# Start of a two-layer hybrid encoder: products of ones ahead on TensorE, a full-row norm spread, one transfer queue, and the second token tile's split ahead of k's casts

## The chip, the cores and the metric

The kernel runs on one core of a Trainium2 chip. The metric is the device time of one execution in microseconds (us). The kernel before took 761.21 us (median of 3 executions, 759.78 to 761.6). All places in time below are microseconds from the start of the profiled span.

## The reference

Two layers (`DEPTH` 2) work on 256 tokens of 1024 channels in float32. Each layer normalises its input, projects it with one matrix of 10,272 columns, sends the segments through a gated delta branch and a differential attention branch, merges both and adds the result to the input. A last norm closes it.

```
def rmsnorm(x, w):
    y = xf * lax.rsqrt(jnp.mean(xf * xf, axis=-1, keepdims=True) + EPS)
    return y.astype(x.dtype) * w

for l in range(DEPTH):
    h = rmsnorm(x, norm_w[l])
    proj = h @ w_in[l]                     # q_a k_a v_a ab_a z_a q_b k_b v_b z_b gates
    ...
    x = x + merged @ w_out[l]
return rmsnorm(x, final_norm_w)
```

The change touches only the norm of the tokens and the first projections behind it (`v_b`, the 32 columns `ab_a`, then `k_a`).

## The kernel before, in words

The 256 tokens are two tiles of 128 (`m` = 0 and 1), one token per partition; `xt[i][:, m]` holds half `i` (512 channels) of tile `m`. A projection needs float32 accuracy, so each operand is cut into a rounded part `hi` and a remainder `lo`, and each product is three matmuls (hi·hi, hi·lo, lo·hi). Weights come in pieces `kp` of 256 rows by 512 columns (512 KB): a transfer to `raw` (L249), a cast on ScalarE to `hi` (L253, "CAST") and a subtraction on VectorE to `lo` (L255).

**The norm of one tile** (`normed`, L192). ScalarE squares both halves with a running sum (L189), GpSimd adds the two sums and EPS (L184) and takes the power -0.5 (L185), and VectorE multiplies tokens, this factor and the norm weight (L199, once per half, tile `h_n`). `norm_row` (L159) supplies the norm weight on all partitions for layer 0: it loads one row of 1024 numbers to partition 0 and multiplies it, on TensorE, with a row of ones (`tri[0:1, 0, :]`, the first row of an upper triangle that GpSimd makes at L114 to L116) into two banks `wb` (L165).

**The split of one tile** (`split_T`, L204). TensorE transposes `h_n` in eight blocks (L209, bank `pt_h`), ScalarE copies four at a time to `hT` hi (L215), and VectorE subtracts to `hT` lo (L216).

**The order around the change.** Layer 0 starts with `v_b`, first half of its columns: `proj_by_tile` (L286) runs all 8 `kt` blocks for token tile 0 and then the same 8 for tile 1. The four weight pieces sit in the buffers `wA`, `wktm`, `wvtm` and `wB` (pieces 0 to 3) and are used twice. `between(kt)` (L389) puts the second token tile's transfers and norm among the pieces of the first pass. Behind that come the 16 small products of `ab_a` (`abp`, L503, weights `wabr`, L498 and L499) and `k_a` (`proj_fm`, L314, banks `pf_k`, weights `hi_k` and `lo_k`).

A scheduler fixes the order on each engine when the program is built. `behind(ins)` and `tc.issue_after(ins)` keep an instruction behind another; `later[kp]` does this for the cast and the subtraction of piece `kp`, `mark["later"]` for those of the next `proj_fm`, and `held[kp]` for its transfer, which then goes to ScalarE's queue if the instruction it is held behind runs there. Each engine works strictly in its order. `raw` has three buffers in turn; pieces named in `spare` take one of two others instead. SyncE (SP) issues the transfers of its queue in order and waits where a buffer isn't free yet.

Of the kernel before, what the change touches and what calls it, by code (L numbers as in the profile page):

```python
# [17 lines left out]
P = 128  # L18
# [31 lines left out]
def hybrid_encoder(  # L50
# [108 lines left out]
    def norm_row(w_row, nm):  # L159

        row = work.tile([P, DM], F32, tag="w4c", name=f"wr_{nm}", bufs=4)
        nc.scalar.dma_start(out=row[0:1, :], in_=w_row.unsqueeze(0))
        wb = [bank(f"wb_{nm}{i}") for i in range(2)]
        for i in range(2):
            T.matmul(wb[i], tri[0:1, 0, :], row[0:1, 512 * i : 512 * i + 512], start=True, stop=True)  # L165
        return wb

    def norm_weights(w_row, nm):
# [9 lines left out]
    def norm_factor(xt_, m, h, r, ss, halves_, after=None):  # L178


        for i in halves_:
            with behind(after):
                sq = mark["square", m, i] = square(xt_, m, h, ss, i)
        G.tensor_scalar(r, ss[:, 0:1], ss[:, 1:2], EPS, ALU.add, ALU.add)  # L184
        mark["pow"] = G.tensor_tensor(r, r, mhalf[:, :1], ALU.pow).ins  # L185
        return sq

# [155 lines left out]


    U_ = big.tile([P, 2, 16, P], F32, name="U_")
    wb = norm_row(norm_w[0], "n0")
    xt = e4("xt0", "ex")
    xdr = x[0].rearrange("(m p) (i d) -> p i m d", p=P, i=2)
# [18 lines left out]
    for l in range(DEPTH):  # L367
# [18 lines left out]
        if l == 0:  # L386
            later[0] = None, mark["norm", 0][1]

            def between(kt):  # L389
                if kt == 2:  # L390
                    held[1] = mark["square", 0, 0]
                    later[1] = mark["split", 0, 0]
                elif kt == 4:
                    tokens(1, mark["square", 0, 1])
                    held[2] = mark["vb00", 0][0]
                elif kt == 6:
                    prenorm(1, xt, wb, 0, (mark["split", 0, 1][0], mark["vb00", 2][1]))
                    later[3] = None, mark["norm", 1][1]
        else:
            later = {1: mark["norm", 0], 2: (mark["norm", 0][0], mark["split", 0, 0][1]), 3: mark["split", 0, 0]}  # L400
            mark["later"] = {0: mark["norm", 1], 1: mark["norm", 1]}
        for _ in proj_by_tile(hT, wl, C_VB, evac_v(0), f"vb{l}0", places, later=later,
                              spare=(1, 3) if l else (), held=held, between=between,
                              turn=lambda m: None if m or not l else mark["turn", 1, 0]):
            pass
        if l == 0:
            norms = mark["pow"]
            with tc.issue_after(norms):
                G.memset(U_, 0.0)
            pos_f = const.tile([P, NM], F32, name="pos_f")  # L410
            with tc.issue_after(mark["norm", 1][1]):
                V.tensor_copy(pos_f, pos_i)
            freq = const.tile([P, RD], F32, name="freq")
            for i, f in enumerate(INV_FREQ):
                V.memset(freq[:, i : i + 1], f)
            angs = const.tile([P, 2, NM, RD], F32, name="angs")
            ang, ang2 = angs[:, 0], angs[:, 1]
            for m in range(NM):
                V.tensor_scalar(ang[:, m, :], freq, pos_f[:, m : m + 1], None, ALU.mult)
            turns = const.tile([P, NM, RD], F32, name="turns")  # L420
            turns_i = const.tile([P, NM, RD], I32, name="turns_i")
            V.tensor_scalar(turns, ang, 1.0 / (2.0 * math.pi), None, ALU.mult)
            V.tensor_copy(turns_i, turns)
            V.tensor_copy(turns, turns_i)
            for c in (TWO_PI_A, TWO_PI_B, TWO_PI_C):
                V.scalar_tensor_tensor(ang, turns, -c, ang, ALU.mult, ALU.add)
            PI_IN = 3.1415925
            V.tensor_scalar(ang, ang, PI_IN, -PI_IN, ALU.min, ALU.max)
            sincos = const.tile([P, 2, NM, RD], F32, name="sincos")
            sin, cos = sincos[:, 0], sincos[:, 1]  # L430
            over = const.tile([P, NM, RD], F32, name="over")
            V.tensor_scalar(ang2, ang, math.pi / 2, None, ALU.add)
            V.tensor_scalar(over, ang2, math.pi, None, ALU.is_gt)
            V.scalar_tensor_tensor(ang2, over, -2.0 * math.pi, ang2, ALU.mult, ALU.add)
            V.tensor_scalar(ang2, ang2, PI_IN, -PI_IN, ALU.min, ALU.max)
# [55 lines left out]


        wab = work.tile([P, KT, 32], F32, tag="w2a", name=f"wab{l}", bufs=2)
        with behind(None if l else mark["vb00", 2][0]):
            (nc.sync if l else nc.scalar).dma_start(
                out=wab, in_=wl[:, C_AB : C_AB + 32].rearrange("(k p) c -> p k c", p=P))
        wabr = work.tile([P, KT, 64], F32R, tag="w2c", name=f"wabr{l}", bufs=3)
        S.copy(wabr[:, :, 0:32], wab)  # L498
        V.tensor_tensor(wabr[:, :, 32:64], wab, wabr[:, :, 0:32].bitcast(F32), ALU.subtract)  # L499
        abp = ps_p.tile([P, 512], F32, tag="p", name=f"abp{l}")  # L500
        for kt in range(KT):
# [700 lines left out]
```

## Time and profile before

| | |
|---|---|
| profiled execution, own time | 761.66 us |
| its span (first to last instruction) | 759.9 us |
| around the span | 1.8 us |
| median of three executions | 761.21 us |
| TensorE busy | 745.7 us, 98% |
| VectorE, ScalarE, GpSimd busy | 575.6, 471.0, 124.2 us |
| moved by DMA | 131.24 MB, 173 GB/s |

PE is TensorE's matmul row, PEld its weight loads, DVE is VectorE, ACT ScalarE, POOL GpSimd and SP SyncE; a "q" behind the name marks an engine's issue of transfers. A row of the timeline has start, length, engine, line, operation, what is written <- what is read, partitions x elements, the count of merged instructions, and in brackets the idle time ahead and what ended it. Float32 matmuls that are not rounded show as two records each (the two products of the norm row are "x4").

### The profile page before, as it was taken

Reading aid. Unit: us, or ns where it says so; the run is one execution under the profiler, and the core shown is the slowest. Engines: PE = TensorE matmul, PEld = TensorE weight load, DVE = VectorE, ACT = ScalarE, POOL = GpSimd, SP = SyncE. Lnnn points to the kernel's source line nnn. Section 1 sums busy time; section 2 is a strip of 40 time slices with the busy share of each in tenths; the row PEclk is TensorE's granted clock in tenths of the full one; section 3 lists DMA queues with packets and bytes.
Section 4 is the critical chain, followed back from the end, with each engine's and each line's share of the span. In section 5 each row is a group of like instructions: output and inputs, shape, how many; then the busy total and the mean of one; then the engine's idle time right before and its main releaser. Section 6 shows DMA issues by size and latency. Waiting matters only on the chain. (4 is left out here: it accounts for less than half of the span.)

```text
span 759.9 us, 13759 instructions
## 1 busy us (share of the span) xinstructions
PE 745.7 (98%) x5158; PEld 640.3 (84%) x5158; DVE 575.6 (76%) x1083; ACT 471.0 (62%) x1012; POOL 124.2 (16%) x187
## 2 busy tenths in 40 slices
PE   7999999999999999999999999999999999999996
PEld 4899889977788889988889889889777888998784
DVE  5686999999886764487577779999989668436782
ACT  5657675667787574645545577665777757465551
POOL 5100451111113130000010025202110410201000
PEclk9999999999999999999999999999999999999999
DMA  7662677776668342557674347768656834335541
GB/s 232 214 204 63 199 225 203 220 199 199 188 195 176 90 137 84 167 192 230 215 228 136 88 140 254 202 195 229 188 167 194 195 113 142 103 111 205 193 139 55
DMA packets 71795, 131.24 MB, mean 173 GB/s; under 512 B 12288, under 2 KB 12752, under 8 KB 71729
## 3 DMA queue, kind: packets, MB, share of 16 engines
q1 hardware_dynamic: 62718, 111.94, 48.8%
q0 software_dynamic: 6304, 15.15, 7.4%
q10 hardware_dynamic: 2706, 3.28, 1.3%
q8 instruction: 40, 0.66, 0.4%
q14 instruction: 27, 0.21, 0.1%
HBM read 123.44 MB, written 6.91 MB: 172 GB/s over the span
## 5 line engine op out<-in xcount | busy, mean ns | idle before, releaser
L270 PE MATMUL pp_qk<-lo_qk,hT 128*128 128x512 f32 x128 | 50.7, 396 | 0.2
L271 PE MATMUL pp_qk<-hi_qk,hT 128*128 128x512 f32 x128 | 50.0, 391 | 0.0
L255 DVE TENSOR_TENSOR lo_qk<-raw_qk,hi_qk 128x1024 fp32r<-128x1024 f32 x32 | 39.6, 1239 | 9.6 <-ACT hi_qk L253 9.3
L269 PE MATMUL pp_qk<-hi_qk,hT 128*128 128x512 f32 x128 | 45.1, 393 | 0.0
L253 ACT CAST hi_qk<-raw_qk 128x1024 fp32r<-128x1024 f32 x28 | 29.4, 1049 | 24.6 <-PE pp_qk L271 12.1
L926 ACT ACTIVATE es<-sc,mx 128x256 f32<-128x256 f32 x64 | 29.7, 475 | 20.7 <-DVE mx L924 20.7
L255 DVE TENSOR_TENSOR lo_pb<-raw_pb,hi_pb 128x1024 fp32r<-128x1024 f32 x16 | 19.6, 1227 | 23.0 <-ACT hi_pb L253 22.9
L327 PE MATMUL pf_q<-hT,hi_q 128*128 128x256 f32 x128 | 36.2, 286 | 0.0
L325 PE MATMUL pf_q<-hT,hi_q 128*128 128x256 f32 x128 | 36.1, 287 | 0.0
L325 PE MATMUL pf_v<-hT,hi_v 128*128 128x256 f32 x128 | 35.9, 285 | 0.0
L327 PE MATMUL pf_v<-hT,hi_v 128*128 128x256 f32 x128 | 35.8, 284 | 0.0
L325 PE MATMUL pf_k<-hT,hi_k 128*128 128x256 f32 x128 | 35.7, 284 | 0.0
L327 PE MATMUL pf_k<-hT,hi_k 128*128 128x256 f32 x128 | 35.6, 283 | 0.0
L255 DVE TENSOR_TENSOR lo_ga<-raw_ga,hi_ga 128x1024 fp32r<-128x1024 f32 x16 | 19.5, 1219 | 20.9 <-ACT hi_ga L253 20.9
L329 PE MATMUL pf_q<-hT,lo_q 128*128 128x256 f32 x128 | 34.8, 285 | 0.0
L329 PE MATMUL pf_v<-hT,lo_v 128*128 128x256 f32 x128 | 34.6, 288 | 0.0
L329 PE MATMUL pf_k<-hT,lo_k 128*128 128x256 f32 x128 | 34.4, 284 | 0.0
L554 DVE SCALAR_TENSOR_TENSOR cvq<-pf_q,cw,cvq 128x254 f32<-128x254 f32 (+1 forms) x64 | 29.9, 477 | 1.9 <-ACT cvq L550 1.4
L253 ACT CAST hi_pa<-raw_pa 128x1024 fp32r<-128x1024 f32 x16 | 16.9, 1054 | 22.8 <-PE pp_pa L271 16.7
L554 DVE SCALAR_TENSOR_TENSOR cvv<-pf_v,cw,cvv 128x254 f32<-128x254 f32 (+1 forms) x64 | 30.0, 476 | 0.1
L554 DVE SCALAR_TENSOR_TENSOR cvk<-pf_k,cw,cvk 128x254 f32<-128x254 f32 (+1 forms) x64 | 28.5, 478 | 2.0 <-ACT cvk L550 1.3
L270 PEld LDWEIGHTS pp_qk<-lo_qk,hT 128*128 128x128 f32 x128 | 24.0, 188 | 6.5 <-DVE lo_qk L255 1.7
(372 smaller groups left out, 2520.2 us busy)
## 6 DMA issues: line engine op xcount, KB each, us to landing
raw_qk<-in_w_in_dram SPq DMA_DIRECT2D x32, 512.0 KB, 4.1
raw_k<-in_w_in_dram SPq DMA_DIRECT2D x16, 512.0 KB, 4.7
raw_q<-in_w_in_dram SPq DMA_DIRECT2D x16, 512.0 KB, 3.8
raw_v<-in_w_in_dram SPq DMA_DIRECT2D x16, 512.0 KB, 3.8
raw_zb<-in_w_in_dram SPq DMA_DIRECT2D x16, 512.0 KB, 3.8
raw_za<-in_w_in_dram SPq DMA_DIRECT2D x16, 512.0 KB, 3.8
raw_ga<-in_w_in_dram SPq DMA_DIRECT2D x16, 512.0 KB, 4.0
raw_pb<-in_w_pb_dram SPq DMA_DIRECT2D x16, 512.0 KB, 4.1
```

The costliest lines, as they stand in the source:

```text
L253: high = (V.tensor_copy if kp in turned else S.copy)(hi[:, :, :n], raw[:, :, :n]).ins
L255: mark[nm, kp] = high, V.tensor_tensor(lo[:, :, :n], raw[:, :, :n], hi[:, :, :n].bitcast(F32), ALU.subtract).ins
L269: T.matmul(o, act[kt // 4][:, 0, kt % 4, ts_], hi, start=kt == 0, stop=False)
L270: T.matmul(o, act[kt // 4][:, 0, kt % 4, ts_], lo, start=False, stop=False)
L271: mark["proj"] = T.matmul(o, act[kt // 4][:, 1, kt % 4, ts_], hi, start=False, stop=kt == KT - 1).ins
L325: T.matmul(o, hi[:, cs], act[kt // 4][:, 0, kt % 4, :], start=first, stop=False, skip_group_check=True)
L327: T.matmul(o, hi[:, cs], act[kt // 4][:, 1, kt % 4, :], start=False, stop=False, skip_group_check=True)
L329: T.matmul(o, lo[:, cs], act[kt // 4][:, 0, kt % 4, :], start=False, stop=done, skip_group_check=True)
L554: V.scalar_tensor_tensor(ca[:, o0:o1], acc[:, b, o0 + sft : o1 + sft], cw[:, j, cb : cb + 1], ca[:, o0:o1], ALU.mult, ALU.add)
L926: S.activation(es[:, n, qt, :], spv[:, qt, :], AF.Exp, bias=mx[:, n, qt : qt + 1], accum_out=s_all[:, h, n, qt : qt + 1])
```

## The change

1. `ones` (128x128, filled on VectorE) and eight float32 products of it with itself stand first on TensorE; nothing reads their bank.
2. The norm row's tile is filled with zeros on VectorE first (128x1024); the row's transfer overwrites partition 0, and the two spreading products take all 128 rows (with the whole `tri[:, 0, :]`, whose column sums give the row again, as all other rows are zero). Both keep their place in the program.
3. The norm's addition of the two sums moves from GpSimd to VectorE (L184). This helper serves both tiles of both layers and the last norm.
4. Second token tile, weight pieces 1 and 2 of `v_b` and the weights `wab` of `ab_a` lose their `held` entries and go to SP's queue. Piece 3 takes a spare buffer, so `raw` starts its second turn one piece later.
5. Piece 2's cast is put behind tile 0's second split; the second tile's squares go behind piece 2's cast alone (its product stays behind piece 2's subtraction), and k's first cast and subtraction, `pos_f` and the cast of `wab` go behind the second tile's last split.

```diff
     def norm_row(w_row, nm):
         row = work.tile([P, DM], F32, tag="w4c", name=f"wr_{nm}", bufs=4)
+        V.memset(row, 0.0)
         nc.scalar.dma_start(out=row[0:1, :], in_=w_row.unsqueeze(0))
...
-            T.matmul(wb[i], tri[0:1, 0, :], row[0:1, 512 * i : 512 * i + 512], start=True, stop=True)
+            mm = T.matmul(wb[i], tri[:, 0, :], row[:, 512 * i : 512 * i + 512], start=True, stop=True)
+            tc.keep_in_program_order(mm)
...
-        G.tensor_scalar(r, ss[:, 0:1], ss[:, 1:2], EPS, ALU.add, ALU.add)
+        V.tensor_scalar(r, ss[:, 0:1], ss[:, 1:2], EPS, ALU.add, ALU.add)
...
+    ones = work.tile([P, P], F32, tag="sqj", name="ones", bufs=1)
+    V.memset(ones, 1.0)
+    idle = bank_c("idle")
+    for _ in range(8):
+        mm = T.matmul(idle[:, :P], ones, ones, start=True, stop=True)
+        tc.keep_in_program_order(mm)
     wb = norm_row(norm_w[0], "n0")
...
                 if kt == 2:
-                    held[1] = mark["square", 0, 0]
                     later[1] = mark["split", 0, 0]
                 elif kt == 4:
-                    tokens(1, mark["square", 0, 1])
-                    held[2] = mark["vb00", 0][0]
+                    tokens(1)
+                    later[2] = mark["split", 0, 1]
                 elif kt == 6:
-                    prenorm(1, xt, wb, 0, (mark["split", 0, 1][0], mark["vb00", 2][1]))
+                    prenorm(1, xt, wb, 0, mark["vb00", 2])
                     later[3] = None, mark["norm", 1][1]
+                    mark["later"] = {0: mark["split", 1, 1]}
...
-                              spare=(1, 3) if l else (), held=held, between=between,
+                              spare=(1, 3) if l else (3,), held=held, between=between,
...
-            with tc.issue_after(mark["norm", 1][1]):
+            with tc.issue_after(mark["split", 1, 1][1]):
                 V.tensor_copy(pos_f, pos_i)
...
-        with behind(None if l else mark["vb00", 2][0]):
-            (nc.sync if l else nc.scalar).dma_start(
-                out=wab, in_=wl[:, C_AB : C_AB + 32].rearrange("(k p) c -> p k c", p=P))
+        nc.sync.dma_start(out=wab, in_=wl[:, C_AB : C_AB + 32].rearrange("(k p) c -> p k c", p=P))
...
-        S.copy(wabr[:, :, 0:32], wab)
+        with behind(None if l else mark["split", 1, 1][0]):
+            S.copy(wabr[:, :, 0:32], wab)
```

What the scheduler makes of it differs from the order before at three places; everything else stands in the same order on every engine, apart from the addition of item 3, which leaves GpSimd and joins VectorE at every norm.

**The first transfers.** SP's queue from its start, before. `xt` are the tokens of tile 0, `raw_vb` the pieces 0 and 3 of `v_b`, `cwr` the convolution weights, `raw_k` the pieces of `k_a`; the tokens of tile 1, pieces 1 and 2 and `wab` stand in ScalarE's queue, among its casts.

```order
L353 DMA xt_0_103<-in_x_dram 128x512
L353 DMA xt_1_104<-in_x_dram 128x512
L249 DMA raw_vb_143<-in_w_in_dram 128x2x512
L439 DMA cwr_264<-in_conv_w_dram 120x128
L249 DMA raw_vb_198<-in_w_in_dram 128x2x512
L249 DMA raw_k_362<-in_w_in_dram 128x2x512
L249 DMA raw_k_392<-in_w_in_dram 128x2x512
```

The same queue of the changed kernel:

```order
L361 DMA xt_0_115<-in_x_dram 128x512
L361 DMA xt_1_116<-in_x_dram 128x512
L251 DMA raw_vb_155<-in_w_in_dram 128x2x512
L251 DMA raw_vb_165<-in_w_in_dram 128x2x512
L361 DMA xt_0_115<-in_x_dram 128x512
L361 DMA xt_1_116<-in_x_dram 128x512
L251 DMA raw_vb_177<-in_w_in_dram 128x2x512
L251 DMA raw_vb_210<-in_w_in_dram 128x2x512
L447 DMA cwr_276<-in_conv_w_dram 120x128
L502 DMA wab_296<-in_w_in_dram 128x8x32
L251 DMA raw_k_374<-in_w_in_dram 128x2x512
```

The second pair of `xt` rows are the tokens of tile 1. All first transfers except the norm row now stand in this one queue, in the order in which they are used; ScalarE's queue keeps the norm row and, later, two pieces of the second half of `v_b`.

**The second token tile.** VectorE's order before, from the subtraction of piece 2 (`wvtm`) to that of k's second piece; `h_n` is the second tile's product, `hT` its split, `wabr` and `angs` are small work for `ab_a` and the rotary angles.

```order
L255 TENSOR_TENSOR wvtm_vb_136<-raw_vb_165,wvtm_vb_136 128x1024
L199 SCALAR_TENSOR_TENSOR h_n_175<-xt_0_103,xr_n_176,wb_n_99 128x512
L199 SCALAR_TENSOR_TENSOR h_n_175<-xt_1_104,xr_n_176,wb_n_100 128x512
L412 CAST pos_f<-pos_i 128x2
L255 TENSOR_TENSOR wB_vb_137<-raw_vb_198,wB_vb_137 128x1024
L499 TENSOR_TENSOR wabr_286<-wab_284,wabr_286 128x8x32
L419 TENSOR_SCALAR angs<-freq,pos_f 128x8
L255 TENSOR_TENSOR lo_k_361<-raw_k_362,hi_k_360 128x1024
L419 TENSOR_SCALAR angs<-freq,pos_f 128x8
L216 TENSOR_TENSOR hT_0_107<-pt_h_184,hT_0_107 128x4x128
L216 TENSOR_TENSOR hT_1_108<-pt_h_191,hT_1_108 128x4x128
L255 TENSOR_TENSOR lo_k_391<-raw_k_392,hi_k_390 128x1024
```

The same stretch of VectorE in the changed kernel:

```order
L257 TENSOR_TENSOR wvtm_vb_148<-raw_vb_177,wvtm_vb_148 128x1024
L186 TENSOR_SCALAR xr_n_188<-xss_n_189 128x1
L201 SCALAR_TENSOR_TENSOR h_n_187<-xt_0_115,xr_n_188,wb_n_111 128x512
L201 SCALAR_TENSOR_TENSOR h_n_187<-xt_1_116,xr_n_188,wb_n_112 128x512
L257 TENSOR_TENSOR wB_vb_149<-raw_vb_210,wB_vb_149 128x1024
L218 TENSOR_TENSOR hT_0_119<-pt_h_196,hT_0_119 128x4x128
L218 TENSOR_TENSOR hT_1_120<-pt_h_203,hT_1_120 128x4x128
L420 CAST pos_f<-pos_i 128x2
L257 TENSOR_TENSOR lo_k_373<-raw_k_374,hi_k_372 128x1024
L427 TENSOR_SCALAR angs<-freq,pos_f 128x8 x2
L257 TENSOR_TENSOR lo_k_403<-raw_k_404,hi_k_402 128x1024
L506 TENSOR_TENSOR wabr_298<-wab_296,wabr_298 128x8x32
```

The split of the second tile moved ahead of `lo_k`, `wabr` and the angles; the norm's addition (L186) now stands on VectorE, behind the subtraction of piece 2. ScalarE's casts follow: the second tile's squares now stand behind the cast of piece 2, the two copies to `hT` ahead of k's casts. On TensorE the order of the two passes stays, but the 16 `abp` products, which stood in three groups among the second pass, now stand in one group behind it.

**The start of layer 1.** VectorE's order before around the norm of tile 1 there (`wB` is a weight piece of `v_b`, `hT_1` the second half of tile 0's split, `lo_k` the first pieces of `k_a`):

```order
L255 TENSOR_TENSOR wB_vb_4130<-raw_vb_4148,wB_vb_4130 128x1024
L216 TENSOR_TENSOR hT_1_4007<-pt_h_4068,hT_1_4007 128x4x128
L199 SCALAR_TENSOR_TENSOR h_n_4100<-xt_0_3924,xr_n_4101,wb_n_4002 128x512
L199 SCALAR_TENSOR_TENSOR h_n_4100<-xt_1_3925,xr_n_4101,wb_n_4002 128x512
L255 TENSOR_TENSOR lo_k_4298<-raw_k_4299,hi_k_4297 128x1024
L255 TENSOR_TENSOR lo_k_4328<-raw_k_4329,hi_k_4327 128x1024
L216 TENSOR_TENSOR hT_0_4006<-pt_h_4109,hT_0_4006 128x4x128
```

And in the changed kernel:

```order
L257 TENSOR_TENSOR wB_vb_4142<-raw_vb_4160,wB_vb_4142 128x1024
L218 TENSOR_TENSOR hT_1_4019<-pt_h_4080,hT_1_4019 128x4x128
L186 TENSOR_SCALAR xr_n_4113<-xss_n_4114 128x1
L201 SCALAR_TENSOR_TENSOR h_n_4112<-xt_0_3936,xr_n_4113,wb_n_4014 128x512
L201 SCALAR_TENSOR_TENSOR h_n_4112<-xt_1_3937,xr_n_4113,wb_n_4014 128x512
L257 TENSOR_TENSOR lo_k_4310<-raw_k_4311,hi_k_4309 128x1024
L257 TENSOR_TENSOR lo_k_4340<-raw_k_4341,hi_k_4339 128x1024
L218 TENSOR_TENSOR hT_0_4018<-pt_h_4121,hT_0_4018 128x4x128
```

Only the addition joined the row; it comes behind the subtraction for `hT_1` in VectorE's queue, where GpSimd had it in a queue of its own.

## The prediction

> **What bounds the kernel now.** I read the page's busy times first, then the busy times by stage, then the timeline of the first 28 us. From the page:
>
> ```profile
> PE 745.7 (98%) x5158; PEld 640.3 (84%) x5158; DVE 575.6 (76%) x1083; ACT 471.0 (62%) x1012; POOL 124.2 (16%) x187
> ```
>
> And by stage (length, then the busy time of PE, PEld, DVE, ACT and POOL, the clock, the DMA share and GB/s):
>
> ```profile
> 0.00:28.00 28.00, 22.86 (x87) 15.52 (x87) 15.62 (x40) 15.12 (x26) 12.62 (x26) 1.00 0.76 237
> 28.00:380.00 352.00, 351.69 (x2489) 304.77 (x2488) 273.47 (x515) 225.72 (x489) 54.57 (x78) 1.00 0.60 177
> 380.00:392.00 12.00, 11.82 (x61) 9.30 (x60) 11.59 (x14) 7.36 (x12) 2.14 (x4) 1.00 0.65 192
> ```
>
> From 28 to 380 us TensorE is idle for 0.3 us of 352, and the order there is unchanged but for the norm's addition. So whatever the change gains or loses before the first product of `k_a` moves the rest of layer 0 as a whole. The idle time to be had stands in the first 28 us, and a busy PE there is not yet one at full pace. The timeline of the first tile:
>
> ```profile
> 0.80 0.52 ACTq L162 DMA_DIRECT2D wr_n<-in_norm_w_dram  x1
> 0.86 0.26 DVE L415 MEMSET freq<- 128x1 f32 x8 [0.86 <-PEq L1190]
> 1.35 1.28 ACT L189 ACT_TABLE_LOAD   x1 [1.35 <-PEq L1190]
> 3.10 3.78 PE L165 MATMUL wb_n<-wr_n,tri 1*128 1x512 f32 x4 [3.10 <-POOL tri L116]
> 3.85 0.63 ACT L189 ACTIVATE h_n<-xt 128x512 f32<-128x512 f32 x1 [1.21 <-DMA xt<-in_x_dram]
> 5.32 0.30 POOL L184 TENSOR_SCALAR xr_n<-xss_n 128x1 f32<-128x1 f32 x1 [2.03 <-ACT h_n L189]
> 5.71 0.57 POOL L185 TENSOR_TENSOR xr_n<-xr_n,mhalf 128x1 f32<-128x1 f32 x1
> 6.31 1.41 DVE L199 SCALAR_TENSOR_TENSOR h_n<-xt,xr_n,wb_n 128x512 f32<-128x512 f32 x2 [3.22 <-POOL xr_n L185]
> 7.69 1.04 ACT L253 CAST wA_vb<-raw_vb 128x1024 fp32r<-128x1024 f32 x1 [2.48 <-DMA raw_vb<-in_w_in_dram]
> 8.77 1.23 DVE L255 TENSOR_TENSOR wA_vb<-raw_vb,wA_vb 128x1024 fp32r<-128x1024 f32 x1 [1.05 <-ACT wA_vb L253]
> 9.28 3.45 PE L309 MATMUL pp_vb<-wA_vb,hT 128*128 128x512 f32 x6 [0.20 <-ACT hT L215]
> 9.91 0.68 DVE L216 TENSOR_TENSOR hT<-pt_h,hT 128x512 fp32r<-128x512 f32 x1
> ```
>
> The first projection waits for piece 0 of its weights (7.69), whose cast and subtraction end at 10.0. The second tile:
>
> ```profile
> 12.15 1.03 ACT L253 CAST wvtm_vb<-raw_vb 128x1024 fp32r<-128x1024 f32 x1
> 13.22 1.23 DVE L255 TENSOR_TENSOR wvtm_vb<-raw_vb,wvtm_vb 128x1024 fp32r<-128x1024 f32 x1 [0.82 <-ACT wvtm_vb L253]
> 14.36 1.40 DVE L199 SCALAR_TENSOR_TENSOR h_n<-xt,xr_n,wb_n 128x512 f32<-128x512 f32 x2
> 15.75 1.22 DVE L255 TENSOR_TENSOR wB_vb<-raw_vb,wB_vb 128x1024 fp32r<-128x1024 f32 x1
> 17.02 1.42 PE L309 MATMUL pp_vb<-wB_vb,hT 128*128 128x512 f32 x5
> 18.88 1.22 DVE L255 TENSOR_TENSOR lo_k<-raw_k,hi_k 128x1024 fp32r<-128x1024 f32 x1 [0.38 <-ACT hi_k L253]
> 19.39 0.73 PE L309 MATMUL pp_vb<-wA_vb,hT 128*128 128x512 f32 x2 [0.94 <-ACT hT L215]
> 20.16 1.28 DVE L216 TENSOR_TENSOR hT<-pt_h,hT 128x512 fp32r<-128x512 f32 x2
> 20.90 1.19 PE L309 MATMUL pp_vb<-wA_vb,hT 128*128 128x512 f32 x4 [0.66 <-DVE hT L216]
> 21.93 1.54 PE L309 MATMUL pp_vb<-wktm_vb,hT 128*128 128x512 f32 x6
> 27.08 0.97 PE L503 MATMUL abp<-hT,wabr 128*64 128x256 f32 x7
> 27.88 0.28 PE L325 MATMUL pf_k<-hT,hi_k 128*128 128x256 f32 x1
> ```
>
> The second pass begins at 19.39 and stalls again at 20.90, both times for `hT`, which stands behind `lo_k` (18.88) on VectorE. That is the wait that item 5 removes.
>
> **The second pass: the first term.** The first pass ends about 18.3 (five products from 17.02, some 0.25 apart). From there to the first `pf_k` product at 27.88 pass 9.6 us. The work in it is 24 products, spaced (1.54 - 0.39) / 5 = 0.23, so 5.5; the small transpose of `cwr`, some 0.1; and 16 `abp` products, spaced (0.97 - 0.28) / 6 = 0.115, so 1.85. Together 7.45, beside which nothing else runs on TensorE. If nothing waits any more, `pf_k` starts at 25.75: **2.1 us gained**, provided `wB` is subtracted no later than now.
>
> Is it? VectorE's row decides. Its operations follow one another at 1.14 (`wA` 8.77 to `hT` 9.91), 0.6 (`hT`, 1.28 for two of 0.68) and 0.67 (`h_n`, 1.41 for two). First its start. The zero fill is new, and no row shows VectorE filling 128x1024: between the 0.26 of eight tiny fills and the 1.23 of a subtraction of that size I take 1.15, since its size is the latter's. With 0.2 for `ones` ahead of it, from 0.86 on, it ends at 2.2. The norm row's transfer on ScalarE waits for it (2.2, not 0.80), and behind it stand the table load and the squares: 2.2 + 0.52 + 1.28 = 4.0, against 3.85 when the tokens let the first square start. Cost 0.2, and the norm factor is ready at about 6.35 instead of 6.28, because the addition takes 0.2 on VectorE instead of 0.30 and a hand-over.
>
> TensorE: the four records of the norm row take 3.78, so a float32 product of 512 columns takes 1.7 at this pace and one of 128 columns 0.43. Eight take 3.4, from 1.1 to 4.5. The row has landed by then: now PE's first wait ends with `tri`, not with the row, so it needed at most 3.10 - 0.80 = 2.3; 2.2 + 2.3 = 4.5. The spread ends at 4.5 + 3.4 + 0.2 = 8.1 at the present pace (now 6.9), and VectorE's second `h_n` starts at 8.15, not 7.0. From there: `wA` 8.8, `hT` 9.95, `wktm` 10.6, `hT` 11.7, `wvtm` 12.35, now 13.22. That gain is spent at once: the addition for tile 1 now queues behind `wvtm` (13.5 to 13.75), the power follows on GpSimd (13.85 to 14.4), and `h_n` starts at 14.45, now 14.36. `wB` comes at 15.8, now 15.75, `hT` at 16.9 and 17.55, now 20.16. So the bound on the first pass stays and the second pass is free: 2.1.
>
> For `wvtm` at 12.35 piece 2 must have landed by 11.25. Ahead of it and in it stand five transfers of 0.52 MB, 2.62 MB. In the present trace:
>
> ```profile
> 0.00:11.20 11.20, 7.67 (x15) 3.80 (x16) 4.36 (x14) 5.90 (x10) 3.37 (x14) 1.00 0.73 238
> ```
>
> 238 GB/s over 11.2 us are 2.67 MB, so it lands just in time, at about 11.0. k's two pieces and `wab` make 4.4 MB, 18.5 us at this rate; their casts and subtractions, with `wabr` last, end near 21.5, and `abp` needs `wabr` at 23.9, so k's later casts cost nothing while that 2 us cover lasts. The conversion of `wab` is hidden by the same cover. The tokens of tile 1, pieces 1 and 2 are moved past `cwr` in SP's queue; `cwr` now lands behind 3.2 MB, near 14, and its transpose is due in the second pass, after 18.
>
> **The clock.** TensorE's pace changes between two rows of the same eight transposes:
>
> ```profile
> 7.12 1.97 PE L209 MATMUL pt_h<-ident,h_n 128*128 128x128 f32 x8 [0.24 <-DVE h_n L199]
> 16.04 1.04 PE L209 MATMUL pt_h<-ident,h_n 128*128 128x128 f32 x8
> ```
>
> The page prints full clock for both, but the first runs at half pace, although the one-row products had kept PE busy from 3.10. If the products of ones bring the full pace as they end, the spread takes 1.7 instead of 3.4 and ends at 6.4; if not, 8.1 holds. The Trainium skill, "TensorE: Matmul & The Clock Gate", Part 1, has the clock open after one busy window of about 3.4 us that runs freely; by that rule it opens between 4.5 and 7.9 here, and the trace agrees on the factor of two, but has no row that tells the moment. An earlier spread gives up to 0.75 more, but only if piece 2 is also earlier (10.4). I take 0.2 of it: **first term 2.3**, ends -3.7 and 2.9 (rivals).
>
> **The addition at layer 1: the second term.**
>
> ```profile
> 385.09 0.44 POOL L184 TENSOR_SCALAR xr_n<-xss_n 128x1 f32<-128x1 f32 x1 [5.91 <-ACT h_n L189]
> 385.28 0.68 DVE L216 TENSOR_TENSOR hT<-pt_h,hT 128x512 fp32r<-128x512 f32 x1
> 386.22 1.42 DVE L199 SCALAR_TENSOR_TENSOR h_n<-xt,xr_n,wb_n 128x512 f32<-128x512 f32 x2 [0.26 <-POOL xr_n L185]
> 390.56 0.77 PEld L309 LDWEIGHTS pp_vb<-wA_vb,hT 128*128 128x128 f32 x4 [0.38 <-DVE hT L216]
> ```
>
> GpSimd adds at 385.09 beside VectorE's `hT`. On VectorE the addition comes behind `hT`: 385.9 to 386.1, power 386.2 to 386.77, `h_n` 386.8, 0.58 later. Behind it queue k's two subtractions and the `hT` for which PE already waits at 390.56. **Cost 0.5**, between 0 (if a later wait swallows it) and 0.6.
>
> **The end: the third term.** Nothing hides the last norm:
>
> ```profile
> 753.70 0.19 ACT L189 ACTIVATION_READ_ACCUMULATOR h_nf<-xt 128x1 f32 x1
> 753.99 0.30 POOL L184 TENSOR_SCALAR xr_nf<-xss_nf 128x1 f32<-128x1 f32 x1 [4.42 <-ACT h_nf L189]
> 18.28 0.23 DVE L419 TENSOR_SCALAR angs<-freq,pos_f 128x8 f32<-128x8 f32 x1
> ```
>
> VectorE's like operation takes 0.23 against 0.30, and it starts 0.03 behind ScalarE (`wA`: 8.74 to 8.77) where GpSimd needs 0.10. **Gain 0.15**, between 0.1 and 0.2.
>
> **Sum.** 2.3 - 0.5 + 0.15 = 1.95. The profiled execution would take 761.66 - 1.95 = 759.7. It lay 0.45 above the median 761.21; against that the sum gives 759.3.
>
> **The rivals.**
>
> More comes through: the full pace opens early and piece 2 lands at 10.4. Then `wvtm` goes at 11.5, `h_n` of tile 1 at 13.6, and the first term is 2.9; with 0.3 at layer 1 the sum is 2.75: 758.5. For it: item 4 takes competing transfers away from pieces 0 to 2. Against it: the same bytes stand ahead of piece 2, and no row shows full-row products this early. By the rule of the Trainium skill above, its first half is likely.
>
> Piece 2 comes no sooner than now (cast at 12.15 without a wait before it). Then the addition behind `wvtm` moves `h_n` to 15.2, 0.85 later than now: first term 1.25, sum 0.9: 760.3.
>
> **Slower:** the norm row lands late. It now is issued at 2.2 into ScalarE's queue while SP's queue holds six transfers. ScalarE's queue in the present trace, issue to landing:
>
> ```profile
> raw_vb<-in_w_in_dram ACTq DMA_DIRECT2D x4, 512.0 KB, 8.1
> xt<-in_x_dram ACTq DMA_DIRECT2D x2, 256.0 KB, 5.8
> ```
>
> At 5.8 it lands at 8.0, 3.5 after the ones are done; all that follows moves by 3.5: 2.1 - 3.5 - 0.5 + 0.15 = -1.75, so 763.0; at 8.1 it is 765.3. The gain is gone from a landing at 6.25. Against it: the row has 4 KB, those had 256 and 512.
>
> **Chances.** Forecast 0.42; more comes through 0.38; piece 2 late 0.12; norm row late 0.08. About 0.3% (2.3 us) is what a measurement of this kernel can tell from no change. The forecast lies just inside, and a small part of it counts as faster: faster 0.40, within 0.53, slower 0.07. The range takes in the second case's far end and the third: 757.6 to 761.4.
>
> **What the changed profile would show.** The second pass without an idle bracket, and `pf_k` at 25 to 26: first term right. `h_n` of tile 1 near 14.4 behind its addition: right; at 13.6 or below, the second case; above 15, the third. The spread's first product at 4.5: the norm row was in time; at 6 or later, the slower case. A wait of PE for `hT` of about 0.9 instead of 0.38 near 390: second term right. The forecast is wrong if `abp` waits for `wabr`, or if TensorE waits for `lo_k` between 26 and 36, which would give the gain back.

## The result, and the profile after

| | before | after |
|---|---|---|
| median (20 executions each) | 761.08 us | 762.01 us |
| lowest to highest | 759.78 to 762.68 us | 760.97 to 764.2 us |
| ratio, 95% interval | | 1.0014 [1.0008, 1.0021] |
| profiled execution, own time | 761.66 us | 764.2 us |
| its span | 759.9 us | 762.4 us |

The change costs 0.9 us; a gain of 1.95 us was forecast (759.3 us). The profiled execution of the changed kernel is the longest of its twenty, so its start shows the loss at its largest: the two other kernels with the same late norm row (runs 3 and 9 below) begin the spread of the row at 5.48 and 5.59 in their profiles, not at 8.87. First the page's busy line, then the three stages of before, each moved by the 2.1 us by which `pf_k` now comes later (columns as before: length, busy time of PE, PEld, DVE, ACT, POOL, clock, DMA share, GB/s):

```profile
PE 746.8 (98%) x5174; PEld 642.0 (84%) x5174; DVE 577.9 (76%) x1091; ACT 471.3 (62%) x1012; POOL 121.4 (16%) x181
```

```profile
0.00:30.10 30.10, 23.78 (x102) 17.26 (x103) 16.66 (x44) 14.61 (x24) 11.95 (x24) 0.94 0.77 235
30.10:382.10 352.00, 351.78 (x2490) 304.89 (x2489) 274.08 (x516) 226.35 (x491) 54.48 (x77) 1.00 0.59 176
382.10:394.10 12.00, 11.38 (x59) 8.87 (x58) 11.01 (x15) 7.81 (x12) 1.65 (x3) 1.00 0.71 193
```

The middle is as full as it was, so the loss lies in the first row: TensorE stood 6.3 us idle in 30.1, before 5.1 in 28.0, although 16 records of ones are now counted as busy. The third row holds 0.4 us more idle time. The timeline of the start says what came late:

```profile
1.11 3.78 PE L352 MATMUL idle<-ones 128*128 128x128 f32 x16 [1.11 <-DVE ones L349]
1.22 0.91 DVE L162 MEMSET wr_n<- 128x1024 f32 x1 [0.16 <-issue]
2.16 0.53 ACTq L163 DMA_DIRECT2D wr_n<-in_norm_w_dram  x1
7.94 1.04 ACT L255 CAST wA_vb<-raw_vb 128x1024 fp32r<-128x1024 f32 x1 [2.58 <-DMA raw_vb<-in_w_in_dram]
8.87 3.65 PE L166 MATMUL wb_n<-wr_n,tri 128*128 128x512 f32 x4 [3.98 <-DMA wr_n<-in_norm_w_dram]
10.95 0.75 DVE L201 SCALAR_TENSOR_TENSOR h_n<-xt,xr_n,wb_n 128x512 f32<-128x512 f32 x1 [5.34 <-PE wb_n L166]
13.22 1.22 DVE L257 TENSOR_TENSOR wA_vb<-raw_vb,wA_vb 128x1024 fp32r<-128x1024 f32 x1
14.90 1.07 ACT L255 CAST wvtm_vb<-raw_vb 128x1024 fp32r<-128x1024 f32 x1
15.85 0.65 ACT L191 ACTIVATE h_n<-xt 128x512 f32<-128x512 f32 x1
16.48 0.63 ACT L191 ACTIVATE h_n<-xt 128x512 f32<-128x512 f32 x1
16.69 1.22 DVE L257 TENSOR_TENSOR wvtm_vb<-raw_vb,wvtm_vb 128x1024 fp32r<-128x1024 f32 x1
17.82 0.21 DVE L186 TENSOR_SCALAR xr_n<-xss_n 128x1 f32<-128x1 f32 x1
18.70 1.41 DVE L201 SCALAR_TENSOR_TENSOR h_n<-xt,xr_n,wb_n 128x512 f32<-128x512 f32 x2 [0.67 <-POOL xr_n L187]
20.02 1.22 DVE L257 TENSOR_TENSOR wB_vb<-raw_vb,wB_vb 128x1024 fp32r<-128x1024 f32 x1
```

The bracket at 8.87 is the first thing to see: the ones end at 4.9, and TensorE then waits 3.98 for the 4 KB norm row, issued at 2.16. Everything behind stands in VectorE's strict order: the first `h_n` at 10.95 (6.31 before), `wA`'s subtraction at 13.22 though its cast had begun at 7.94 and took 1.04. `h_n` of tile 1 comes at 18.70, not 14.36. TensorE's rows from the second pass on:

```profile
22.56 1.52 PE L311 MATMUL pp_vb<-wA_vb,hT 128*128 128x512 f32 x6
23.92 1.52 PE L311 MATMUL pp_vb<-wktm_vb,hT 128*128 128x512 f32 x6
...
26.78 1.54 PE L311 MATMUL pp_vb<-wB_vb,hT 128*128 128x512 f32 x6
28.16 1.99 PE L510 MATMUL abp<-hT,wabr 128*64 128x256 f32 x16
29.98 0.28 PE L327 MATMUL pf_k<-hT,hi_k 128*128 128x256 f32 x1
```

(`pp_vb` are the products of `v_b`.) No bracket is left: the idle time that item 5 was to remove is gone (29.98 - 22.56 = 7.42), but the pass starts 3.2 later than the 19.39 of before. At layer 1, and at the last norm:

```profile
387.79 0.21 DVE L186 TENSOR_SCALAR xr_n<-xss_n 128x1 f32<-128x1 f32 x1
388.67 1.41 DVE L201 SCALAR_TENSOR_TENSOR h_n<-xt,xr_n,wb_n 128x512 f32<-128x512 f32 x2 [0.67 <-POOL xr_n L187]
389.57 0.63 PE L211 MATMUL pt_h<-ident,h_n 128*128 128x128 f32 x4 [0.45 <-DVE h_n L201]
393.01 0.77 PEld L311 LDWEIGHTS pp_vb<-wA_vb,hT 128*128 128x128 f32 x4 [0.38 <-DVE hT L218]
```

```profile
756.34 0.19 ACT L191 ACTIVATION_READ_ACCUMULATOR h_nf<-xt 128x1 f32 x1
756.56 0.21 DVE L186 TENSOR_SCALAR xr_nf<-xss_nf 128x1 f32<-128x1 f32 x1 [0.79 <-ACT h_nf L191]
757.45 0.75 DVE L1177 SCALAR_TENSOR_TENSOR h_nf<-xt,xr_nf,wb_n 128x512 f32<-128x512 f32 x1 [0.67 <-POOL xr_nf L187]
```

The transposes of layer 1 and the last product in the kernel before:

```profile
387.12 0.63 PE L209 MATMUL pt_h<-ident,h_n 128*128 128x128 f32 x4
...
754.98 0.75 DVE L1170 SCALAR_TENSOR_TENSOR h_nf<-xt,xr_nf,wb_n 128x512 f32<-128x512 f32 x1 [1.85 <-POOL xr_nf L185]
```

TensorE's new wait at layer 1 is the 0.45 for `h_n` ahead of the transposes, which waited for nothing before; the wait for `hT` that the prediction named stays at 0.38. At the end, from the start of ScalarE's read of the sum to the last product pass 1.11 us (757.45 - 756.34), before 1.28 (754.98 - 753.70).

### The profile page after: what moved, and what is told of

Its sections match the earlier page's. It is cut to its first block, busy times and chain, and to the rows that moved or that the text cites. A ratio compares the mean times of both kernels' runs of the same rounds, so it can differ in the third digit from the quotient of the medians.

```text
span 762.4 us, 13790 instructions
## 1 busy us (share of the span) xinstructions
PE 746.8 (98%) x5174; PEld 642.0 (84%) x5174; DVE 577.9 (76%) x1091; ACT 471.3 (62%) x1012; POOL 121.4 (16%) x181
## 4 chain that ended last, share of the span: by engine, by line
PE 85%; DVE 7%; DMA 3%; issue 3%; ACT 1%; POOL 0%; SPq 0%; POOLq 0%; DVEq 0%; ACTq 0%
PE pp_vb L311 4%; PE pp_qk L272 3%; PE pp_qk L273 3%; PE pp_qk L271 3%; PE pp_za L272 2%; PE pf_v L327 2%; PE pp_gb L272 2%; PE pf_v L331 2%; PE pp_gb L271 2%; PE pf_v L329 2%; PE pp_ga L271 2%; PE pp_za L271 2%; PE sc L923 2%; PE pp_za L273 2%; PE pp_ga L273 2%
## 5 line engine op out<-in xcount | busy, mean ns | idle before, releaser
L561 DVE SCALAR_TENSOR_TENSOR cvv<-pf_v,cw,cvv 128x254 f32<-128x254 f32 (+1 forms) x64 | 30.1, 478 | 0.1
```

The costliest lines, as they stand in the source:

```text
L561: V.scalar_tensor_tensor(ca[:, o0:o1], acc[:, b, o0 + sft : o1 + sft], cw[:, j, cb : cb + 1], ca[:, o0:o1], ALU.mult, ALU.add)
```

## The experiments

Twelve kernels, each timed in 6 to 12 executions beside the kernel before, whose median was 761.0 to 761.2 each time. An interval reaches 0.5 to 1.1 us to either side, so steps of half a us rest on the profiles as well, by two marks. A profile, too, is one execution. The first is the place of the first product of `k_a` (`pf_k`). The second is, at layer 1, the stretch from the first `pp_vb` product to the first `pf_k` product. Each transfer of a piece is moved by sixteen DMA engines, and the trace records the end of each engine's share; "landing" is the last of the sixteen, and the "median engine" is the ninth to end.

| kernel | time | ratio [95%] | wA cast | wvtm cast | h_n tile 1 | pf_k | layer 1 stretch |
|---|---|---|---|---|---|---|---|
| before | 761.08 | 1 | 7.69 | 12.15 | 14.36 | 27.88 | 7.25 |
| changed kernel | 762.01 | 1.0014 [1.0008, 1.0021] | 7.94 | 14.90 | 18.70 | 29.98 | 7.80 |
| 1 row early | 761.54 | 1.0004 [0.9996, 1.0012] | 9.35 | 13.60 | 16.79 | 28.06 | 7.79 |
| 2 one-row spread | 761.77 | 1.0008 [1.0000, 1.0016] | 8.82 | 13.02 | 16.22 | 27.52 | 7.79 |
| 3 addition on GpSimd | 762.09 | 1.0013 [1.0002, 1.0025] | 9.37 | 13.49 | 16.85 | 28.17 | 7.26 |
| 4 both 1 and 3 | 760.98 | 1.0000 [0.9991, 1.0008] | 9.84 | 13.92 | 17.29 | 28.59 | 7.25 |
| 5 second tile ahead of k, alone | 758.60 | 0.9972 [0.9961, 0.9982] | 7.81 | 12.19 | 14.41 | 25.79 | 7.25 |
| 6 one queue, alone | 762.45 | 1.0016 [1.0008, 1.0025] | 8.34 | 13.15 | 15.38 | 28.49 | 7.26 |
| 7 as 4, squares early | 760.40 | 0.9989 [0.9979, 0.9999] | 8.63 | 12.77 | 14.99 | 26.59 | 7.25 |
| 8 as 4, positions late | 760.42 | 0.9990 [0.9981, 0.9999] | 8.67 | 12.80 | 16.17 | 27.49 | 7.25 |
| 9 change without one queue | 761.13 | 1.0003 [0.9995, 1.0012] | 7.68 | 12.01 | 15.51 | 26.80 | 7.80 |
| 10 as 5, with ones and full rows | 759.13 | 0.9976 [0.9965, 0.9987] | 7.86 | 12.65 | 14.87 | 26.16 | 7.24 |
| 11 one piece ahead | 762.11 | 1.0008 [0.9999, 1.0016] | 9.05 | 13.14 | 15.35 | 29.10 | 7.25 |
| 12 as 5, piece 3 early | 760.55 | 0.9991 [0.9977, 1.0005] | 7.81 | 13.25 | 15.47 | 26.74 | 7.25 |

The stretches that no kernel touches (`pf_k` to layer 1) differ by up to 1.2 us between single executions (354.05 to 355.23), which is why a profiled execution alone cannot rank two kernels half a us apart.

### 1 to 4: the late row and the addition

Run 1 loads the norm row at once into a tile of its own and copies it into the zero-filled one:

```diff
-        nc.scalar.dma_start(out=row[0:1, :], in_=w_row.unsqueeze(0))
+        first = work.tile([P, 2, 512], F32, tag="w4a", name=f"wf_{nm}", bufs=2)
+        nc.scalar.dma_start(out=first[0:1], in_=w_row.rearrange("(o i d) -> o i d", o=1, i=2))
+        V.tensor_copy(row[0:1, :], first[0:1].rearrange("p i d -> p (i d)"))
```

> The changed kernel, but the norm row is loaded to a tile of its own from 0.8 us on and copied by VectorE into the zero-filled tile, so that its transfer waits for nothing. Theory (the norm row's late landing behind SP's queue is what turned the first term of the prediction around, and the free second pass does give its 2.1 us): the spread starts near 4.5 instead of 8.9, the first pf_k product at 25 to 26, the time 1.5 to 2.5 us under the kernel before. Rival (the second pass only moved its waits elsewhere, or the row was late because of the fill itself): pf_k not before 27.5, the time within 0.7 us of the kernel before.

```profile
4.69 2.56 PE L168 MATMUL wb_n<-wr_n,tri 128*128 128x512 f32 x4
9.35 1.04 ACT L257 CAST wA_vb<-raw_vb 128x1024 fp32r<-128x1024 f32 x1 [4.42 <-DMA raw_vb<-in_w_in_dram]
```

The spread follows the ones without a wait, and the time falls by only 0.47, within the intervals; `pf_k` stays at 28.06, as the rival had it. Now ScalarE waits 4.42 for piece 0. So the late row alone is not the loss: behind it stood another wait, for the weights.

Run 2 takes the one-row spread of before and no zero fill, and so also issues the row at once (`tri[0:1, 0, :]` and `row[0:1, ...]`, no `V.memset(row, 0.0)`).

> The changed kernel with the one-row spread of before: no zero fill, the transfer at 0.8 us, products of one row; the products of ones stay. Theory (landing alone): as with the early row and full rows, 1.5 to 2.5 us under the kernel before. Rival (the full rows matter because they keep TensorE's full pace): the one-row products after the ones let the pace fall back, the first tile runs at half pace until some 13 us, and the time is 0.5 to 1 us above that of the early row with full rows.

761.77 is within the interval of run 1, and neither the theory nor the rival came true: full rows or one row, the pieces come late (8.82, 13.02).

Run 3 gives the addition back to GpSimd, run 4 does so on top of run 1:

```diff
-        V.tensor_scalar(r, ss[:, 0:1], ss[:, 1:2], EPS, ALU.add, ALU.add)
+        G.tensor_scalar(r, ss[:, 0:1], ss[:, 1:2], EPS, ALU.add, ALU.add)
```

> The changed kernel with the norm's addition back on GpSimd, nothing else. Theory (the addition costs 0.5 us at layer 1 and some 0.4 us at tile 1 of layer 0, and gives 0.15 us at the end): 0.5 to 0.9 us under the changed kernel, and PE's wait for hT near 390 us as short as before. Rival (VectorE's addition is hidden): within 0.3 us of the changed kernel.

> Early norm row by a copy, full rows, and the addition back on GpSimd. If both causes are separate and add, 2 to 3.2 us under the kernel before; if the addition hides once the row is early, the same as the early row alone.

Run 3 shows nothing in its time (762.09, its rival's); run 4 against run 1 gives 0.56, still within the intervals. The stretch at layer 1 is clearer than the times: 7.79 or 7.80 in all four kernels with the addition on VectorE, 7.24 to 7.26 in all ten with it on GpSimd. The addition costs 0.55 there. With the row early and the addition back, the change is still not faster than before (760.98; neither case of run 4's expectation came true), so there is a further loss of the size of item 5's gain.

### 5: the second tile ahead of k's casts, alone

```diff
+                    mark["later"] = {0: mark["split", 1, 1]}
...
-            with tc.issue_after(mark["norm", 1][1]):
+            with tc.issue_after(mark["split", 1, 1][1]):
                 V.tensor_copy(pos_f, pos_i)
...
-        S.copy(wabr[:, :, 0:32], wab)
+        with behind(None if l else mark["split", 1, 1][0]):
+            S.copy(wabr[:, :, 0:32], wab)
```

> The kernel before with item 5's later part alone: the second token tile's copies and subtractions ahead of k's casts, and wabr's conversion behind them; two queues, one-row spread, the addition on GpSimd and the second tile's squares as before. Theory (the second pass gains its idle 2.1 us, and the change lost it ahead of the second pass, by later landings, a later norm row and squares behind piece 2's cast): the first pass is that of before, the second pass starts near 18.5 and has 7.45 of work, the first product of k_a comes at 25.8 to 26.0 (27.88 in the kernel before), and the time is about 759.0 (758.8 to 759.4). Rival (the second pass cannot run free, since k's pieces or wabr are late once their casts stand behind): the first product of k_a or the products for lo_k wait, the time is 760.5 to 761.5.

```profile
17.09 1.43 PE L309 MATMUL pp_vb<-wB_vb,hT 128*128 128x512 f32 x5
18.36 1.55 PE L309 MATMUL pp_vb<-wA_vb,hT 128*128 128x512 f32 x6
...
25.79 0.28 PE L325 MATMUL pf_k<-hT,hi_k 128*128 128x256 f32 x1
```

The first pass is that of before (17.09, before 17.02), the second runs without a wait, `pf_k` comes 2.09 earlier, and the median is 2.4 to 2.5 below that of before (1.4 to 3.0 by the interval; 2.1 were predicted for this item). This is the fastest of all kernels here, faster than the kernel before and than the changed one: item 5's gain is real, and the rest of the change gives it away.

### 6, 11 and 12: a transfer queued behind another

Run 6 is the kernel before with item 4 alone (the holds of pieces 1 and 2 and of tile 1's tokens removed, `spare=(3,)`, `wab` on SP). Run 11 moves one transfer, by dropping `held[1]`: piece 1 goes into SP's queue behind piece 0, at 2.16 instead of 3.86 in ScalarE's. Run 12 is run 5 with piece 3 in a tile of its own, issued in ScalarE's queue 0.4 behind piece 2:

```diff
-                              spare=(1, 3) if l else (), held=held, between=between,
+                              spare=(1, 3) if l else (3,), held=held, between=between,
...
-                    later[3] = None, mark["norm", 1][1]
+                    later[3] = 2, mark["norm", 1][1]
+                    held[3] = mark["vb00", 0][0]
```

> The kernel before with item 4 alone: the weight pieces, tokens and wab in SP's one queue in the order of use; one-row spread, norm row in ScalarE's queue at once, splits and squares as the kernel before orders them except for the holds that went with the queue. Theory (in one deep queue a transfer lands with the slowest of its 16 DMA engines while the fast ones run ahead, so each piece lands later): piece 0's last engine ends at 8 to 9.8, not 7.67, piece 2's at 12.9 to 13.9, not 12.05; the second tile's normalization and the second pass come 0.5 to 2 us later; time 761.6 to 763. Rival (the order of use makes pieces 0 to 2 earlier, as the prediction had it for its second case): piece 2 lands at 10.4 to 11.2, time 760.3 to 761.1.

> The kernel before with one transfer moved: weight piece 1 issued behind piece 0 in SP's queue at about 2.2 instead of 3.86 in ScalarE's; all else as before. Theory (every transfer put early behind another in the queue lets the DMA engines that are done first run on into it, and the one ahead lands later): the cast of wA 0.2 to 0.8 later than 7.69, the rest of the chain of tile 1 much as before, time 761.0 to 761.6. Rival (only the whole queue of seven does it): wA at 7.7, time 760.9 to 761.2.

> The kernel of the run with item 5's later part alone (758.6) with weight piece 3 in a tile of its own, issued in ScalarE's queue right behind piece 2 (at 8.2 instead of 10.1). wB's subtraction at 15.8 bounds its first pass. Theory (a held transfer that starts 1.9 earlier lands earlier): wB's cast 0.5 to 1 earlier than 14.73, the second pass up to 0.7 earlier than 18.36, time 757.9 to 758.5. Rival (the engines share what there is and piece 2 or k's pieces pay for it): wvtm's cast later than 12.4, time 758.6 to 759.4.

Run 6, by stage over the first 11.2 us, and two rows of its timeline (the profiled execution, 761.13, is the shortest of its eleven):

```profile
0.00:11.20 11.20, 7.04 (x14) 3.16 (x14) 3.80 (x13) 5.08 (x8) 3.37 (x14) 1.00 0.79 252
```

```profile
8.34 1.04 ACT L253 CAST wA_vb<-raw_vb 128x1024 fp32r<-128x1024 f32 x1 [3.33 <-DMA raw_vb<-in_w_in_dram]
...
13.15 1.05 ACT L253 CAST wvtm_vb<-raw_vb 128x1024 fp32r<-128x1024 f32 x1
```

252 GB/s are more than the 238 of before, and piece 2 still lands 1.1 later, as the theory had it. The ends of the sixteen shares say how. Piece 2: median engine 11.26 before, 11.00 here; last engine 12.05 before, 13.13 here. The engines that are done with a piece run on into the next, which stands ready in the queue: the first share of piece 3 ends at 11.87 here, ahead of piece 2's last, and at 13.12 before, behind it. The slowest engine is 2.1 behind the median instead of 0.8, and the cast waits for it. Most of this lag stands at piece 0 already. From piece 0 to piece 2 it is 2.7, 2.0 and 2.1 here; before, where pieces 1 and 2 are held, it falls from 1.8 to 1.0 and 0.8. The trace does not name the engine of a share.

All fourteen profiles agree on piece 0. It lands at 7.66 to 7.83 in the five kernels that issue piece 1 only at 3.8 to 4.0, in ScalarE's queue (before, runs 5, 9, 10 and 12), and at 7.92 to 9.81 in the nine that put piece 1 right behind it. Run 11's row and run 12's:

```profile
9.05 1.04 ACT L253 CAST wA_vb<-raw_vb 128x1024 fp32r<-128x1024 f32 x1 [4.11 <-DMA raw_vb<-in_w_in_dram]
```

```profile
13.25 1.05 ACT L253 CAST wvtm_vb<-raw_vb 128x1024 fp32r<-128x1024 f32 x1 [1.15 <-DMA raw_vb<-in_w_in_dram]
...
14.54 1.05 ACT L253 CAST wB_vb<-raw_vb 128x1024 fp32r<-128x1024 f32 x1 [0.25 <-DMA raw_vb<-in_w_in_dram]
```

One piece put behind piece 0 delays piece 0 by 1.4 in the profiled execution (7.69 to 9.05), not by 0.2 to 0.8; the eleven times fall into two groups, five from 760.75 to 761.4 and six from 762.1 to 762.75, and the profiled one is of the later group. Run 12, which was to gain up to 0.7, loses 2: piece 3, issued 1.9 earlier, comes 0.2 earlier, and piece 2 ahead of it 1.06 later. Its rival was right about the cast of `wvtm`, and the time is above even the rival's 758.6 to 759.4; its twelve times are wide apart (758.05 to 763.1), so 2 is no exact price. The three runs show the same trade: a piece put early gains 0.2 at most (run 11's piece 1 lands at 10.30, before at 9.46), and the one ahead of it, which is waited for, loses 0.65 to 1.4.

### 7 and 8: what else stood in run 4

Run 7 puts the second tile's squares ahead of piece 2's cast again, run 8 moves the transfer of the positions (256 values of 4 bytes, GpSimd's queue) from the start to behind the norms. Both stand on run 4.

```diff
-                    prenorm(1, xt, wb, 0, mark["vb00", 2])
+                    prenorm(1, xt, wb, 0, (mark["split", 0, 1][0], mark["vb00", 2][1]))
```

> The changed kernel with the norm row loaded early and the addition on GpSimd (the run before this one on that, 760.98), and now also the second tile's squares ahead of piece 2's cast on ScalarE. Theory (the squares behind piece 2's cast hold the second tile's normalization, 17.29 there with the subtraction of wvtm done at 16.2): h_n of tile 1 about 1.0 earlier, 16.3, the first product of k_a at 27.6 to 27.9, time 760.0 to 760.4. Rival (the second tile is held by wB's piece, not by its norm): h_n moves, the second pass does not, time 760.8 to 761.2.

> The same base (norm row early, addition on GpSimd, 760.98) with the transfer of the token positions (4-byte elements) moved on GpSimd from the start to behind the two norm factors. Theory A (that transfer of small elements makes some DMA engines lag, and a piece lands with its slowest engine): piece 0's last engine ends at 7 to 8 instead of 9.81, piece 2's at 11.5 to 12.5 instead of 13.90, the second pass starts 1.3 to 2 earlier, time 759.0 to 759.8. Theory B (the lag comes from the depth of the one queue alone): the last engines stay at 9.3 to 9.9 and 13.5 to 14, time 760.8 to 761.2.

Run 4's rows, then those of run 7:

```profile
13.92 1.04 ACT L257 CAST wvtm_vb<-raw_vb 128x1024 fp32r<-128x1024 f32 x1 [1.12 <-DMA raw_vb<-in_w_in_dram]
14.87 0.63 ACT L193 ACTIVATE h_n<-xt 128x512 f32<-128x512 f32 x1
...
17.29 1.41 DVE L203 SCALAR_TENSOR_TENSOR h_n<-xt,xr_n,wb_n 128x512 f32<-128x512 f32 x2 [1.06 <-POOL xr_n L189]
```

```profile
11.49 0.64 ACT L193 ACTIVATE h_n<-xt 128x512 f32<-128x512 f32 x1
...
12.77 1.04 ACT L257 CAST wvtm_vb<-raw_vb 128x1024 fp32r<-128x1024 f32 x1
...
14.99 1.40 DVE L203 SCALAR_TENSOR_TENSOR h_n<-xt,xr_n,wb_n 128x512 f32<-128x512 f32 x2
```

In run 4 `h_n` follows the cast of `wvtm` by 3.37, in run 7 by 2.22: with the squares behind the cast, the norm of tile 1 starts only once piece 2 has landed. That is 1.15 of wait (1.06 of it in run 4's bracket); the other 1.15 by which `h_n` moved is piece 2's earlier landing, which this edit does not explain. Run 8 bears out neither of its theories: pieces 0 and 2 land at 8.64 and 12.78, in run 7, with the positions early, at 8.61 and 12.75, and piece 2's last engine is 2.1 behind the median without them. So the small elements are not what makes engines lag. With these equal landings runs 7 and 8 differ in the profile by the squares and the positions: `h_n` of tile 1 at 14.99 and 16.17, `pf_k` at 26.59 and 27.49, 0.9 apart. Their medians are the same, though, 0.6 below run 4's, all within the intervals: in the times the price of the squares is not settled.

### 9 and 10: the rest of the sum

Run 9 is the changed kernel with item 4 undone, run 10 is run 5 with the ones, the zero fill, the full rows and run 1's early load, and with item 5's hold on piece 2's cast, which leaves ScalarE's order there as in run 5.

> The changed kernel with item 4 alone undone (pieces 1 and 2, the second tile's tokens and wab back in ScalarE's queue with their holds, piece 3 in the pool of three). Theory (the one queue costs 1.4 us, as it did alone, and the costs of the items add up): 762.0 - 1.4 = 760.6, between 760.2 and 761.0; the cast of wA at 7.7 to 8.0 and that of wvtm near 12.2, and the norm row, still issued at 2.2, has landed by 4.5 to 5.5, since fewer transfers stand in the other queue. Rival (the late norm row carries the loss, the queue only stretches transfers that are waited for anyway): the spread still starts at 5 to 9 and the time stays at 761.6 to 762.2.

> The kernel of the run with item 5's later part alone (758.6) with the products of ones and the spread by full rows added, the norm row being loaded at once into a tile of its own and copied into the zero-filled one. Theory (neither the ones nor the full rows matter, since the first projection waits for piece 0 at 7.7 and no clock is gained that lasts): 758.4 to 759.0. Rival 1 (full pace for the first tile's transposes brings the first pass forward): below 758.2. Rival 2 (the clock that opens early closes again in TensorE's wait for the weights, and the first pass runs at half pace for longer): the first product of k_a later than 26.2, time 759.2 or more.

Run 9:

```profile
5.59 3.74 PE L166 MATMUL wb_n<-wr_n,tri 128*128 128x512 f32 x4 [0.69 <-DMA wr_n<-in_norm_w_dram]
7.68 1.04 ACT L255 CAST wA_vb<-raw_vb 128x1024 fp32r<-128x1024 f32 x1 [2.32 <-DMA raw_vb<-in_w_in_dram]
...
10.03 1.22 DVE L257 TENSOR_TENSOR wA_vb<-raw_vb,wA_vb 128x1024 fp32r<-128x1024 f32 x1
```

Pieces 0 and 2 are cast as before (7.68, 12.01), and `pf_k` comes 3.2 earlier than in the changed kernel. The row, issued at 2.17, has landed at 5.45, and the late spread alone now holds `wA`'s subtraction (10.03, before 8.77). 761.13 lies a little above the expected 760.2 to 761.0; the queue is worth 0.9 here, 1.4 alone, neither to better than the intervals.

Run 10, 759.13, is 0.5 above run 5, in between its theory and its second rival and within both intervals. Its spread runs at full pace, but nothing comes of it, since `wA` cannot be cast before 7.86:

```profile
4.65 1.88 PE L168 MATMUL wb_n<-wr_n,tri 128*128 128x512 f32 x4
```

### The sum, one step at a time

The kernels form a chain of small steps: before 761.1; item 5's later part 758.60 (-2.5); ones and full rows with the early load, run 10, 759.13 (+0.5); the one queue, run 7, 760.40 (+1.3); the squares behind piece 2's cast, run 4, 760.98 (+0.6); the addition on VectorE, run 1, 761.54 (+0.6); the row's transfer behind the zero fill, the changed kernel, 762.01 (+0.5). The steps of half a us are each within what the intervals leave open, and are taken for real only where a profile shows them (the layer 1 stretch, the squares, the late spread); the ones' step is shown by none. The first is clear. In the times the queue's sign is clear in run 6 alone; the landings of piece 0 bear it out.

## Why the prediction was wrong

**The second pass: right.** 7.45 of work were predicted, 7.42 and 7.43 (run 5) measured, and `pf_k` at 25.75 is run 5's 25.79. The condition attached to it, "provided `wB` is subtracted no later than now", is what failed: 20.02 instead of 15.75 in the profiled execution, 16.3 to 18.6 in the other kernels with one queue.

**The step that failed first: "238 GB/s over 11.2 us are 2.67 MB, so it lands just in time, at about 11.0".** That is when the median engine ended piece 2 (11.23 in the changed kernel). The last ended at 12.87, in the eight kernels with one queue between 12.75 and 13.90, always later than the 12.05 of before. A mean rate says when the bytes have been moved, not when one transfer is whole. The forecast's second rival ("Piece 2 comes no sooner than now") had the direction, but stopped at "no sooner", and piece 0, on which the whole first pass waits, was not priced as late at all. Item 4 cost 0.9 to 1.4 in the medians (the changed kernel against run 9, run 7 against run 10, run 6 against before), where no cost was counted.

**The second: "The row has landed by then: ... it needed at most ... 2.3".** The bound came from an issue at 0.80, where the row's packet moved at 1.71, ahead of the first packet of the tokens at 1.80, and the row took 1.4. Issued at 2.16, beside a queue of tokens and pieces, it took 3.2 in run 3, 3.3 in run 9 and 6.6 in the profiled execution. The slower rival had the mechanism and, for a landing at 8.0, 763.0; the landing at 8.74 goes with 764.2. In the medians the late row is worth 0.5 (the changed kernel against run 1) or 1.1 (run 3 against run 4, with the addition on GpSimd), both within the intervals. The ones, too, took longer than the 3.4 of the working: 3.78, to 4.9.

**The third was not there at all:** item 5 also puts the squares of tile 1 behind piece 2's cast. The working followed VectorE's row and put the addition behind `wvtm`; ScalarE's row, one engine further up, was not followed. Its price is 0.6 in the chain and 0.9 in the profiles of runs 7 and 8, and is not settled.

**The second term: right in size** (0.5; 0.55 measured), wrong in place: it is paid as the 0.45 ahead of the transposes, not as a longer wait for `hT`. **The third term: right** (0.15; from 1.28 to 1.11, 0.17).

**The clock.** By stage in the changed kernel (the column behind POOL is the granted clock):

```profile
5.60:8.90 3.30, 0.03 (x1) 0.06 (x1) 0.01 (x1) 0.96 (x1) 0.57 (x1) 1.00 0.86 285
9.00:12.30 3.30, 3.30 (x4) 1.12 (x5) 0.75 (x1) 0.00 (x0) 0.00 (x0) 0.50 1.07 376
12.40:20.00 7.60, 6.81 (x32) 4.51 (x30) 6.77 (x9) 5.14 (x9) 1.89 (x2) 1.00 0.59 165
```

The records put the opening at 5.54, within the 4.5 to 7.9 that the prediction took, but TensorE had nothing to do: it closed at 8.96, just as the spread began, and opened again at 12.37. In this execution the full pace that the ones bought fell wholly into the wait for the row. The Trainium skill, "TensorE: Matmul & The Clock Gate", Part 1, has the clock fall back to half after one idle window of about 3.4 us; the trace agrees (8.96 - 5.54 = 3.42).

## What to carry to other kernels

When the first product waits for a transfer, do not put the next large one right behind it in its queue. The kernels here whose first piece landed on time held the second back by two us. Order of use in one deep queue kept the byte rate and still delayed each landing, which is set by the slowest of the engines. Predict a landing from the last engine of a like transfer under like traffic, never from a mean rate, and never carry a small transfer's time from the quiet start of a kernel to a busy stretch. And when an edit moves several engines' work behind a landing, follow each engine's row, then test each item alone: here one part of one item was worth 2.5 us in the medians, and the rest of the change cost 3.4.

## What the runs showed of the hardware

- The norm row's 4 KB moved in 0.16 us once they began, at 8.05 in the changed kernel, 5.9 us after the issue; in the kernel before they moved in 0.19 us, from 1.71, 0.9 after the issue. It is the start that waits, in a stretch in which the DMA engines move other transfers at 249 GB/s (0 to 11.2 us).
- Of the sixteen engines that share a 512 KB piece, the last ends 0.5 to 1.0 us behind the median for piece 2 where piece 3 is not queued right behind it (before, runs 5 and 9 to 11), 1.6 to 2.7 where it is (the changed kernel and runs 1 to 4 and 6 to 8), and 1.8 in run 12. What makes the slow ones slow stays open; it is not the transfer of 4-byte elements (run 8).
- With ones that keep TensorE busy from 1.1 the clock records begin with an opening at 4.2 to 6.3 (in run 9 only at 9.2), without them at 13.2 to 16.8. Run 10 beside run 5 shows no gain from it, since the first projection waits for its weights.
